# A hybrid decoder layer in one kernel: pair splits inside the next attention step, tied side sums, tied index score units, and query doubling on ScalarE

## The chip, the cores and the metric

The kernel runs on one core of a Trainium2 chip. A core has TensorE (PE, with its weight loads shown apart as PEld), VectorE (DVE), ScalarE (ACT), GpSimd (POOL) and SyncE (SP), which here issues the transfers. The metric is the device time of one execution in microseconds (us).

## The reference, cut to what matters

One decoder layer on `x` of 1024 tokens by 1024 channels, all in float32: a modulated norm, one wide input projection, sparse attention with an index that picks 256 keys for each query, retention, a gated merge, an output projection, and a gated feed-forward of width 2816.

```python
h = _rmsnorm(x, norm1_w) * (1.0 + scale1) + shift1
proj = jnp.dot(h, w_in)
(qa, ka, va, iq, ik, iw, qr, kr, vr, gr, ga, gb) = jnp.split(proj, ...)
...
# index: 8 heads of 64, blocks of 128 queries
s_h = jnp.einsum('bqhd,bsd->bqhs', iqb, ikf) * idx_scale
score = jnp.einsum('bqh,bqhs->bqs', iwb * w_scale, jax.nn.relu(s_h))
score = jnp.where(causal[None], score, NEG)
_, idx = lax.top_k(score, topk)
...
logits = jnp.einsum('bqhd,bqkhd->bqhk', qb, kg) * att_scale
p = jax.nn.softmax(jnp.where(valid[:, :, None, :], logits, NEG), axis=-1)
att = jnp.einsum('bqhk,bqkhd->bqhd', p, vg)
y_a = jnp.dot(att, w_attn_proj)
ret = _retention(_rotate(qr), _rotate(kr) * HEAD_DIM_RK ** -0.5, vr)
y_r = jnp.dot(jax.nn.silu(gr) * _head_groupnorm(ret, gn_w), w_ret_proj)
merged = jax.nn.sigmoid(ga) * y_a + jax.nn.sigmoid(gb) * y_r
x = x + gate1 * jnp.dot(merged, w_out)
...
ffn = jnp.dot(jax.nn.silu(jnp.dot(h2, w_ffn_gate)) * jnp.dot(h2, w_ffn_up), w_ffn_down)
x = _rmsnorm(x + gate2 * ffn, final_norm_w)
```

## The kernel before

**Products.** Each float32 operand of a large product is split in two parts of a reduced type, `hi` by a ScalarE copy and `lo` by a subtraction on GpSimd or VectorE, and a product is three matmuls: hi·hi, hi·lo, lo·hi. Weights are split by `split_weight` (L77 `whi`, L80 `wlo`), after a load by SyncE into `wraw`; `rows_slot` loads and splits one slot of 128 rows. `mm_tok` (lines L126, L128, L129) makes the three matmuls for each of the eight slots of a token tile of 128 rows. The later stages add and subtract blocks of the operands first and so save some products; the sums that this takes on the weights are the "side sums" (`raws` in `early_factors`, L1601, and `dw` of the down projection, L1771).

**Order.** A scheduler orders the instructions of every engine by priority and readiness; each engine then runs its own queue in that order. `turns_after(a, b)` ties `a` behind `b` on their engine without a wait. `in_line` ties each of the attention's instructions behind the one written before it on the same engine.

**The index score stage (about 104 to 213 us).** For each block of 128 queries from the third on, and for two groups of four heads, the queries `iqk` are doubled into `iqd` (L590: one half by VectorE, one by GpSimd; a single buffer), transposed on TensorE (L593) into a PSUM tile `tr`, and split to `qst` (L595 ScalarE, L596 VectorE). A score unit is a pair of matmuls for one head and up to 512 keys (L603, L604) into one of three `lg` banks; ScalarE takes the relu into one of three `rl` (L607) and VectorE adds it to the score (L611). There are 80 units. They are tied among the products of the projection of V, unit `11 * (8 t + k) // 8 - 16` behind product k of tile t, and the last ones are left to the scheduler. VectorE also makes the modulation there (`macc`, L704 and L706, fed by loads `mw`). Behind V follows the q, k projection of retention: eight tiles, each with four ScalarE copies `qk` (L833) and rotations by GpSimd (L840 to L846), and then retention's value tiles (`vs`, L902), with weight slots of their own.

**The attention (about 818 to 921 us).** The steps go over four pairs of heads, four steps each. In step d TensorE makes the logits of step d (L1315, `lga`) and, among them, five groups of transposes of the probabilities of step d − 1 (L1399, `tra`, two banks; copied to `pt` by ScalarE L1404, the third group by VectorE L1402), then the products with V (L1419, `pva`). VectorE takes the maxima (L1318), ScalarE the exponentials (L1327). When a pair's last step is through, its two output halves `pva` are split: `aT_hi` (L1423, ScalarE) and `aT_lo` (L1424, VectorE), both halves at once, directly behind the products.

**The merge (about 925 to 970 us).** For eight output blocks `nt`, products `ya` and `yb`, VectorE's gate products `sg` (L1512) and sums `merged` (L1513); then `split_merged` (`mhi` L1542, `mlo` L1543) and the products with `w_out`, whose sums VectorE adds to `x1` (L1631). After token tile 2 of the first half, `early_factors` loads and prepares the first blocks of the feed-forward's weights, with four VectorE subtractions (L1601).

**The down projection.** Products of the feed-forward's `c` (L1013, L1713: made on VectorE from the accumulators) run between those of its weights; a list `todo` of side sums (L1771) is emptied two tasks per step of the sequence.

## Time and profile before

| | us |
|---|---|
| median of three runs | 1700.72 |
| lowest, highest | 1698.78, 1701.47 |
| the profiled execution, own time | 1701.26 |
| its span | 1699.3 |
| granted TensorE clock, mean | 0.998 |
| TensorE busy | 1665.2 (98%) |
| VectorE busy | 1223.5 (72%) |
| GpSimd busy | 863.9 (51%) |
| ScalarE busy | 754.9 (44%) |

A row of the timeline gives start, duration, engine, line, operation, the tiles out<-in with their size, how many in a row, and in brackets how long the engine stood idle before it and what ended that. TensorE's matmuls are pipelined: each 128x512 matmul shows some 0.39 us but the next starts 0.23 us behind it.

### The profile page before, as it was taken

Reading aid. Unit: us, or ns where it says so; the run is one execution under the profiler, and the core shown is the slowest. Engines: PE = TensorE matmul, PEld = TensorE weight load, DVE = VectorE, ACT = ScalarE, POOL = GpSimd, SP = SyncE. Lnnn points to the kernel's source line nnn. Section 1 sums busy time; section 2 is a strip of 40 time slices with the busy share of each in tenths; the row PEclk is TensorE's granted clock in tenths of the full one; section 3 lists DMA queues with packets and bytes.
Section 4 is the critical chain, followed back from the end, with each engine's and each line's share of the span. In section 5 each row is a group of like instructions: output and inputs, shape, how many; then the busy total and the mean of one; then the engine's idle time right before and its main releaser. Section 6 shows DMA issues by size and latency. Waiting matters only on the chain.

```text
span 1699.3 us, 24532 instructions
## 1 busy us (share of the span) xinstructions
PE 1665.2 (98%) x8275; PEld 1388.9 (82%) x8275; DVE 1223.5 (72%) x2045; ACT 754.9 (44%) x1464; POOL 863.9 (51%) x854
## 2 busy tenths in 40 slices
PE   7999999999999999999999999999999999999998
PEld 5887878888888887888888788888888888888887
DVE  7639797897995779885665857966655566687674
ACT  4635533343553444431686246633333333445444
POOL 4581294793442787040355730145455545666673
PEclk9999999999999999999999999999999999999999
DMA  9454505512432464963854710235544443676652
GB/s 305 165 175 135 159 26 151 168 43 65 127 124 94 137 189 156 330 161 144 194 127 168 285 47 1 69 118 178 182 143 143 166 144 137 212 277 228 208 159 100
DMA packets 178654, 260.71 MB, mean 153 GB/s; under 512 B 13712, under 2 KB 109408, under 8 KB 176224
## 3 DMA queue, kind: packets, MB, share of 16 engines
q1 hardware_dynamic: 178272, 258.85, 48.6%
q8 instruction: 65, 1.06, 0.2%
q14 instruction: 61, 0.50, 0.1%
q10 hardware_dynamic: 256, 0.30, 0.1%
HBM read 192.51 MB, written 66.58 MB: 152 GB/s over the span
## 4 chain that ended last, share of the span: by engine, by line
PE 85%; DVE 6%; DMA 3%; ACT 2%; issue 2%; POOL 1%; SPq 0%; POOLq 0%; DVEq 0%; ACTq 0%
PE ya L1032 4%; PE ya L1030 4%; PE ya L1034 4%; PE mm L128 4%; PE mm L129 4%; PE mm L126 4%; PE yb L1030 3%; PE yb L1034 3%; PE yb L1032 3%; PE ya L1915 3%; PE ya L1913 3%; PE ya L1914 3%; PE mm L1034 2%; PE mm L1030 2%; PE mm L1032 2%
## 5 line engine op out<-in xcount | busy, mean ns | idle before, releaser
L80 POOL TENSOR_TENSOR wlo<-wraw,whi 128x512 fp32r<-128x512 f32 (+1 forms) x93 | 127.7, 1385 | 123.5 <-ACT whi L77 118.7
L642 DVE TENSOR_SCALAR_CACHE_REDUCE eq<-score,cand 128x384 uint8<-128x384 f32 (+2 forms) x192 | 180.9, 942 | 3.7
L945 POOL TENSOR_TENSOR flo<-tmp,fhi 128x512 fp32r<-128x512 f32 x79 | 107.9, 1366 | 140.5 <-ACT fhi L944 98.5
L126 PE MATMUL mm<-whi,hT_hi 128*128 128x512 f32 (+1 forms) x408 | 156.2, 388 | 1.8 <-ACT qk L833 1.8
L128 PE MATMUL mm<-wlo,hT_hi 128*128 128x512 f32 (+1 forms) x408 | 154.8, 381 | 0.5 <-DVE wlo L80 0.5
L129 PE MATMUL mm<-whi,hT_lo 128*128 128x512 f32 (+1 forms) x408 | 154.0, 380 | 0.0
L1030 PE MATMUL ya<-hc,fhi 128*128 128x512 f32 x344 | 133.8, 390 | 1.4 <-DVE c L1013 1.4
L1032 PE MATMUL ya<-hc,fhi 128*128 128x512 f32 x344 | 133.9, 389 | 0.6 <-DVE hc L1550 0.6
L1034 PE MATMUL ya<-hc,flo 128*128 128x512 f32 x344 | 132.9, 389 | 0.0
L1889 ACT ACTIVATE dslot<-draw 128x512 fp32r<-128x512 f32 x143 | 84.6, 627 | 91.8 <-DMA draw<-act_d 30.4
L945 POOL TENSOR_TENSOR flo<-raws,fhi 128x512 fp32r<-128x512 f32 x60 | 87.0, 1456 | 73.0 <-ACT fhi L944 37.9
L1890 DVE TENSOR_TENSOR dslot<-draw,dslot 128x512 fp32r<-128x512 f32 x81 | 88.9, 1133 | 45.4 <-ACT dslot L1889 45.1
L1890 POOL TENSOR_TENSOR dslot<-draw,dslot 128x512 fp32r<-128x512 f32 x62 | 95.7, 1561 | 49.8 <-ACT dslot L1889 42.0
L944 ACT ACTIVATE fhi<-tmp 128x512 fp32r<-128x512 f32 x82 | 51.5, 629 | 111.5 <-PE ya L1032 57.2
L1030 PE MATMUL yb<-hc,fhi 128*128 128x512 f32 x256 | 99.6, 389 | 0.0
L1032 PE MATMUL yb<-hc,fhi 128*128 128x512 f32 x256 | 99.6, 389 | 0.0
L1034 PE MATMUL yb<-hc,flo 128*128 128x512 f32 x256 | 99.4, 389 | 0.0
L77 ACT ACTIVATE whi<-wraw 128x512 fp32r<-128x512 f32 (+1 forms) x94 | 55.7, 609 | 92.1 <-DMA wraw<-in_w_in_dram 39.1
L998 DVE TENSOR_TENSOR tmp<-raws 128x512 f32<-128x512 f32 x40 | 30.6, 768 | 87.0 <-POOL flo L945 87.0
L126 PEld LDWEIGHTS mm<-whi,hT_hi 128*128 128x128 f32 x408 | 76.9, 189 | 13.6 <-ACT qk L833 2.2
L128 PEld LDWEIGHTS mm<-wlo,hT_hi 128*128 128x128 f32 x408 | 77.2, 189 | 12.5 <-DVE wlo L80 0.7
L129 PEld LDWEIGHTS mm<-whi,hT_lo 128*128 128x128 f32 x408 | 76.9, 189 | 12.7
(477 smaller groups left out, 4909.9 us busy)
## 6 DMA issues: line engine op xcount, KB each, us to landing
draw<-act_d SPq DMA_DIRECT2D x70, 256.0 KB
mw<-in_w_ada_dram SPq DMA_DIRECT2D x32, 512.0 KB
act_d<-c SPq DMA_DIRECT2D x58, 256.0 KB
raw<-in_w_in_dram SPq DMA_DIRECT2D x26, 512.0 KB
raws<-in_w_ffn_gate_dram SPq DMA_DIRECT2D x24, 512.0 KB
raws<-in_w_ffn_up_dram SPq DMA_DIRECT2D x24, 512.0 KB
dw<-in_w_ffn_down_dram SPq DMA_DIRECT2D x22, 512.0 KB
dw_d<-dw SPq DMA_DIRECT2D x10, 1024.0 KB
```

What stands on the lines that cost most here:

```text
L77: last_split[0] = ins = nc.scalar.activation(hi[:, :n], raw[:, :n], AF.Copy)
L80: low = (low_eng or nc.gpsimd).tensor_sub(lo[:, :n], raw[:, :n], f32(hi[:, :n]))
L126: ins = nc.tensor.matmul(ps, lhsT=ahi, rhs=whi[:, :n], start=(i == 0), stop=False)
L128: nc.tensor.matmul(ps, lhsT=ahi, rhs=wlo[:, :n], start=False, stop=False)
L129: nc.tensor.matmul(ps, lhsT=alo, rhs=whi[:, :n], start=False, stop=(i == last))
L642: ins = [nc.vector.tensor_scalar(eq[:, :sc.shape[1]], sc, thr[j], None, op0=op, op1=ALU.add, accum_out=cnt[:, j:j + 1]) for j, sc in enume ...
L945: return ins, (eng or nc.gpsimd).tensor_sub(lo, src, f32(hi))
L1030: mm = nc.tensor.matmul(ps, lhsT=whi[:, k, :], rhs=hhi[:, k, :], start=own and k == 0, stop=False, skip_group_check=True)
L1032: nc.tensor.matmul(ps, lhsT=whi[:, k, :], rhs=hlo[:, k, :], start=False, stop=False, skip_group_check=True)
L1034: nc.tensor.matmul(ps, lhsT=wlo[:, k, :], rhs=hhi[:, k, :], start=False, stop=k == 3, skip_group_check=True)
L1889: nc.scalar.activation(slot[:, 0], raw, AF.Copy)
L1890: ins = lo_eng.tensor_sub(slot[:, 1], raw, f32(slot[:, 0]))
```

## The change

Five edits, none of which alters a value that is computed:

1. `iqd` is written by one ScalarE copy of 128x512 in place of the two copies of 128x256 on VectorE and GpSimd.
2. The rule that ties score units behind products runs on into the first tile of the q, k projection, for all units left. Three of that projection's weight slots are issued ahead of V's tiles, the high parts of slots 6 and 7 are tied behind two of the last relus, and those of the first retention value slots behind the copies of q, k tile 2.
3. The attention's splits of a finished pair are written into the next step's plan: `aT_hi` of the two halves (H0, H1) behind the first and the second group of transposes, `aT_lo` (L0, L1) behind the third group and behind the second block of maxima (LB1).
4. `mlo` and the four side sums of `early_factors` are tied behind the merges and behind the additions to `x1`, and `early_factors` is called at token tile 5 in place of 2.
5. The `dw` side sums are tied behind the last additions too, and the last four products of the sequence issue no tasks.

```diff
-            for u, eng in enumerate((nc.vector, nc.gpsimd)):
-                eng.tensor_copy(iqd[:, :, u, :], iv[:, 4 * g:4 * g + 4])
+            nc.scalar.activation(iqd, iv[:, 4 * g:4 * g + 4].unsqueeze(2).to_broadcast([P, 4, 2, HD]), AF.Copy)
...
+    def qk_slot(hp, k):
+        return rows_slot([(w_in, C_QR + 256 * hp, 256), (w_in, C_KR + 256 * hp, 256)], k,
+                         behind=relus[4 * k - 37] if hp == 0 and k > 5 else None)
+
+    first_qk = [qk_slot(0, k) for k in range(3)]
+    def behind_units(mm, t, k):
+        n = 11 * (KT * t + k) // 8 - 16
+        if n >= 0:
+            turns_after(mm, units[min(n, len(units) - 1)])
...
-            mm_tok(ps, hT.lhs(t), slots)
+            for k in range(KT):
+                mm = mm_tok(ps, hT.lhs(t), slots, ks=(k,))
+                if hp == 0 and t == 0:
+                    behind_units(mm, NT, k)
...
-        slots = [rows_slot([(w_in, C_VR + 2 * DV * hp, 2 * DV)], k, low_behind=turned if k > 4 else None)
+        slots = [rows_slot([(w_in, C_VR + 2 * DV * hp, 2 * DV)], k, low_behind=turned if k > 4 else None,
+                           behind=copied if hp == 0 else None)
...
-            in_line(nc.scalar.activation(aT_hi[p][:, ds], pv, AF.Copy), 2)
-            in_line(nc.vector.tensor_sub(aT_lo[p][:, ds], pv, f32(aT_hi[p][:, ds])), 1)
+            ended.append((aT_hi[p][:, ds], aT_lo[p][:, ds], pv))
...
-        plan = T + V if d == len(steps) else (T[:1] + LB0 + T[1:3] + EB0 + LB1 + T[3:] + EB1 + LS0 + LS1 + ES0 + ES1
-                                              + RB1 + RS0 + RS1 + V)
+        plan = T + V if d == len(steps) else (T[:1] + H0 + LB0 + T[1:2] + H1 + T[2:3] + L0 + EB0 + LB1 + L1 + T[3:] + EB1
+                                              + LS0 + LS1 + ES0 + ES1 + RB1 + RS0 + RS1 + V)
...
-    def split_merged(t, gs=(0, 1)):
+    def split_merged(t, gs=(0, 1), behind=None):
...
+            if behind is not None:
+                turns_after(ins, behind)
...
-                nc.vector.tensor_sub(raw[:, :, P:], raw[:, :, P:], raw[:, :, :P])
+                turns_after(nc.vector.tensor_sub(raw[:, :, P:], raw[:, :, P:], raw[:, :, :P]), behind[2 * p + u])
...
-            mm_tok(head[t], split_merged(t, (0,)), slots, ks=range(4))
+            mm_tok(head[t], split_merged(t, (0,), merges[min(4 + t, KT - 1)]), slots, ks=range(4))
...
-                if t == 2:
-                    early_factors()
+                if t == 5:
+                    early_factors((merges[4], merges[5], added[3], added[5]))
...
-                turns_after(nc.vector.tensor_sub(*(dws[p][:, i, :] for i in (to, x, y))), fenv.added)
+                ins = nc.vector.tensor_sub(*(dws[p][:, i, :] for i in (to, x, y)))
+                for last in [fenv.added, *flow[-1].added.values()]:
+                    turns_after(ins, last)
...
+        if i >= len(seq) - 4:
+            return
```

TensorE's row at the end of the V projection and the start of retention's q, k projection; `mm` is the projection's accumulator, `lg` a score unit's. Before, the last products ahead of the end of the units, the last three units, and the first product behind them:

```order
L126 MATMUL mm<-whi,hT_hi_119 128x512
L128 MATMUL mm<-wlo,hT_hi_119 128x512
L129 MATMUL mm<-whi,hT_lo_120 128x512
L603 MATMUL lg<-khi,qst 128x512
L604 MATMUL lg<-klo,qst 128x512
L603 MATMUL lg<-khi,qst 128x512
L604 MATMUL lg<-klo,qst 128x512
L603 MATMUL lg<-khi,qst 128x512
L604 MATMUL lg<-klo,qst 128x512
L126 MATMUL mm<-whi,hT_hi_119 128x512
```

and after, the last unit but one, and the last, with the products between and behind them:

```order
L602 MATMUL lg<-khi,qst 128x512
L603 MATMUL lg<-klo,qst 128x512
L126 MATMUL mm<-whi,hT_hi_119 128x512
L128 MATMUL mm<-wlo,hT_hi_119 128x512
L129 MATMUL mm<-whi,hT_lo_120 128x512
L126 MATMUL mm<-whi,hT_hi_119 128x512
L128 MATMUL mm<-wlo,hT_hi_119 128x512
L129 MATMUL mm<-whi,hT_lo_120 128x512
```

Before, the three units stand together behind two whole q, k tiles; now the last units stand singly among the first tile's products, and the last one ahead of the products of slots 6 and 7 of that tile.

ScalarE's row at the start of the score stage; `whi` are weight splits, `vst` the V tile's copy, `rl` the relus. Before:

```order
L595 ACTIVATE qst<-tr 128x512
L77 ACTIVATE whi<-wraw 128x512 x2
L776 ACTIVATE vst<-mm 128x512
L595 ACTIVATE qst<-tr 128x512
L607 ACTIVATE rl<-lg 128x384
L77 ACTIVATE whi<-wraw 128x512
```

and after:

```order
L594 ACTIVATE qst<-tr 128x512
L589 ACTIVATE iqd<-iqk 128x512
L77 ACTIVATE whi<-wraw 128x512 x2
L785 ACTIVATE vst<-mm 128x512
L594 ACTIVATE qst<-tr 128x512
L589 ACTIVATE iqd<-iqk 128x512
L606 ACTIVATE rl<-lg 128x384
L77 ACTIVATE whi<-wraw 128x512
```

Each copy `iqd` stands directly behind the `qst` of the group before it.

ScalarE's row in the attention step behind a finished pair; `sx` and `sxs` are the exponentials, `pt` the transposed probabilities. Before:

```order
L1327 ACTIVATE sxs,mx<-sxs,mx 128x128 x2
L1423 ACTIVATE aT_hi<-pva 128x512 x2
L1404 ACTIVATE pt<-tra 128x512 x2
L1327 ACTIVATE sx,mx<-sx,mx 128x896
L1404 ACTIVATE pt<-tra 128x512
```

and after:

```order
L1343 ACTIVATE sxs,mx<-sxs,mx 128x128 x2
L1420 ACTIVATE pt<-tra 128x512
L1449 ACTIVATE aT_hi<-pva 128x512
L1420 ACTIVATE pt<-tra 128x512
L1449 ACTIVATE aT_hi<-pva 128x512
L1343 ACTIVATE sx,mx<-sx,mx 128x896
L1420 ACTIVATE pt<-tra 128x512
```

The first copy `pt` moved ahead of both splits, the second between them and the step's first exponential.

## The prediction

> **What bounds the kernel now.** I read the page first: busy times, then the chain that ended last.

> ```profile
> PE 1665.2 (98%) x8275; PEld 1388.9 (82%) x8275; DVE 1223.5 (72%) x2045; ACT 754.9 (44%) x1464; POOL 863.9 (51%) x854
> PE 85%; DVE 6%; DMA 3%; ACT 2%; issue 2%; POOL 1%; SPq 0%; POOLq 0%; DVEq 0%; ACTq 0%
> ```

> TensorE (PE) is busy 98% of the span and carries 85% of the chain; the change takes away none of its matmuls. So a gain can only come from the places where TensorE stands still: 1699.3 − 1665.2 = 34 us, part of it at start-up and the end. Next, the view of the waits, for TensorE alone (waited for: total us, times, longest us):

> ```profile
> PE tra L1399 <- ACT pt L1404: 2.6, 5, 0.9
> ...
> PE tr L593 <- DVE iqd L590: 2.4, 2, 1.9
> ...
> PE mm L1034 <- POOL wlo L945: 1.8, 1, 1.8
> PE mm L126 <- ACT qk L833: 1.8, 1, 1.8
> PE tra L1399 <- DVE pt L1402: 1.7, 4, 0.5
> PE ya L1030 <- DVE c L1013: 1.4, 2, 1.0
> PE lg L603 <- ACT rl L607: 1.2, 1, 1.2
> ...
> PE yb L139 <- DVE sg L1512: 0.3, 1, 0.3
> ```

> All but one of these rows (wlo L945, in a stretch whose order the change leaves alone) is a wait at a place where the change alters the order. They sum to 11.4 us, so that is about the most there is. Five edits, five terms; I went to the timeline at each.

> **Term a, the score stage: queries doubled by ScalarE (ACT).** Twelve pairs of copies to `iqd`, half on VectorE (DVE), half on GpSimd (POOL), become twelve ScalarE copies of 128x512. The timeline at the largest hole, the windows of the stage (the numbers behind the length are busy us of PE, PEld, DVE, ACT, POOL), and the page's row for a ScalarE copy of that size:

> ```profile
> 117.47 0.60 ACT L595 ACTIVATE qst<-tr 128x512 fp32r<-128x512 f32 x1 [1.37 <-PE tr L593]
> 118.23 1.51 DVE L706 SCALAR_TENSOR_TENSOR macc<-mw,colT,macc 128x1024 f32<-128x1024 f32 x1 [0.23 <-DMA mw<-in_w_ada_dram]
> 118.88 0.39 PE L129 MATMUL mm<-whi,hT_lo 128*128 128x512 f32 x1
> 119.67 1.39 DVE L590 COPY iqd<-iqk 128x256 f32<-128x256 f32 x1
> 121.09 0.69 DVE L596 TENSOR_TENSOR qst<-tr,qst 64x512 fp32r<-64x512 f32 x1
> 121.21 0.63 PE L593 MATMUL tr<-ident,iqd 128*128 128x128 f32 x4 [1.93 <-DVE iqd L590]
> ...
> 148.57 0.38 PE L603 MATMUL lg<-khi,qst 128*128 128x256 f32 x1 [1.16 <-ACT rl L607]
> 120.00:140.00 20.00, 18.26 (x92) 15.16 (x93) 17.79 (x28) 12.37 (x25) 5.73 (x8) 1.00 0.56 177
> 140.00:160.00 20.00, 18.84 (x105) 15.88 (x104) 19.75 (x37) 11.28 (x27) 3.17 (x4) 1.00 0.42 132
> L77 ACT ACTIVATE whi<-wraw 128x512 fp32r<-128x512 f32 (+1 forms) x94 | 55.7, 609 | 92.1 <-DMA wraw<-in_w_in_dram 39.1
> ```

> At 118.23 a 1.51-us addition of the modulation's sum holds VectorE; the copy `iqd` comes behind it at 119.67 and takes 1.39; TensorE waits 1.93. After the change the copy stands behind `qst` on ScalarE: 117.47 + 0.60 + 0.61 = 118.68, before TensorE is through with its product of 118.88. What is late next is the lower half of `qst` (0.69) on VectorE, still behind the addition: 118.23 + 1.51 + 0.69 = 120.43. The score unit that reads it then starts some 0.9 us late. The gain there is about 1.2 of 2.1. At the other of the two waits on `iqd` (2.4 − 1.9 = 0.5) I count it all. At 148.57 the wait for a relu goes back to VectorE, whose load in that window is 19.75 of 20; taking copies away from it helps, while ScalarE gets more: I count 0.3 of 1.16. Cost on ScalarE: 12 × 0.61 = 7.3 us over the 50 us from 115 to 161, beside 12.37 and 11.28 busy us of 20, so it lies in its idle time. Term a: 2.0. Ends: +3.5 (the three waits of 1.93, 0.5 and 1.16 all gone) and, since a single `iqd` buffer makes every group's transposes wait for a copy in ScalarE's queue behind relus, below nothing: that is priced among the rivals.

> **Term b, the last ten score units tied into the first q, k tile.** Before, three units stand one behind the other and the next tile's product comes after them. The timeline, and the windows around 213 and around a wait of the same length at 655 (PEclk is the third number from the end):

> ```profile
> 212.52 1.57 ACT L607 ACTIVATE rl<-lg 128x512 f32<-128x512 f32 x3 [1.18 <-PE lg L604]
> 213.00 0.39 PE L604 MATMUL lg<-klo,qst 128*128 128x512 f32 x1
> 213.97 2.19 ACT L833 ACTIVATE qk<-mm,rscale 128x128 f32<-128x128 f32 x8
> 215.18 0.50 PE L126 MATMUL mm<-whi,hT_hi 128*128 128x512 f32 x1 [1.78 <-ACT qk L833]
> 215.20 2.56 POOL L840 TENSOR_TENSOR rra<-qk,cosr 128x512 f32<-128x512 f32 x1 [11.08 <-ACT qk L833]
> ...
> 216.47 0.63 PE L129 MATMUL mm<-whi,hT_lo 128*128 128x512 f32 x1
> ...
> 219.46 0.56 PE L126 MATMUL mm<-whi,hT_hi 128*128 128x512 f32 x1
> 216.00:219.60 3.60, 3.60 (x11) 2.80 (x10) 3.50 (x9) 0.57 (x3) 3.60 (x5) 0.55 0.51 150
> 655.00:657.30 2.30, 0.48 (x4) 0.06 (x2) 2.26 (x6) 0.22 (x1) 2.30 (x3) 1.00 0.49 164
> 657.30:661.00 3.70, 3.70 (x16) 3.09 (x17) 3.70 (x7) 2.28 (x5) 3.70 (x3) 1.00 0.78 235
> 254.20 3.80 POOL L80 TENSOR_TENSOR wlo<-wraw,whi 128x512 fp32r<-128x512 f32 x3
> ```

> ScalarE owes three relus and then the eight `qk` copies of two tiles (2.19); the product at 215.18 needs an accumulator that only these copies free. TensorE, done at 213.00 + 0.23, restarts at 215.18: 1.95 lost. In the new order the last units stand among the products of the first tile, whose copies then come behind few relus, and each later tile (24 products × 0.23 = 5.5 us) gives ScalarE time for four copies (1.1). The wait goes; nothing else on ScalarE is late there. Behind the wait the clock fell: 0.55 in that window, and the seven steps from 216.47 to 219.46 took 2.99 us where 16 matmuls in 3.70 us (0.23 each) would make it 1.61, so 1.4 more. Whether this comes back is not certain: the stop at 655 was as long (1.8 in the waits) and cost no clock. I take it as tied to the pause, since it starts 1.3 us behind it and no other stretch of this stage has it. Term b: 1.95 + 1.4 = 3.4. Ends: 1.5 (the pause only, with 0.4 left) and 3.7.

> [...]

> The same edit puts the first tile's rotation on GpSimd a tile earlier, and some low parts of retention's first weights (L80, 1.27 each by the row of three) between the rotations instead of behind them. Before, GpSimd had these three to do at 254.20, behind the rotations that start at 215.20: 39 us for eight tiles, 4.9 each, against 5.5 on TensorE. The earlier start pays for about 5.5 us of low parts put in between, so I expect no wait of the value tiles; a rival below prices it.

> **Term c, the attention pairs' splits.** Windows of one ordinary step and of two steps in which a finished pair is split, and the split:

> ```profile
> 858.11:864.61 6.50, 6.50 (x68) 5.75 (x67) 4.28 (x16) 4.79 (x11) 2.28 (x4) 1.00 0.89 208
> 864.61:872.64 8.03, 6.72 (x67) 5.75 (x66) 5.47 (x19) 6.44 (x16) 4.20 (x5) 1.00 1.02 218
> 892.30:900.48 8.18, 6.84 (x70) 5.82 (x70) 5.75 (x21) 6.58 (x17) 4.22 (x6) 1.00 0.12 42
> 867.81 1.06 ACT L1423 ACTIVATE aT_hi<-pva 128x512 fp32r<-128x512 f32 x2
> ```

> The latter two are 1.53 and 1.68 longer than the first, and TensorE stands idle for 1.31 and 1.34 of it, because both `aT_hi` (1.06 together) stand on ScalarE ahead of both `pt` copies, and both `aT_lo` on VectorE ahead of the logits' maxima. Three such steps lose nearly 4 us together (the two rows of `pt` waits in the first view, 4.3, hold them and some of the last step). After, one `pt` comes ahead of each `aT_hi`, and each `aT_lo` stands behind a `pt` or a maximum. But ScalarE's work in those steps, 6.44 and 6.58, is about the whole of an ordinary step, so not all closes: a step can come down to about 6.8–7.0. Term c: 0.5 + 2 × 1.0 = 2.5; ends 1.0 and 3.5. The last pair's splits stand behind the last step as before: nothing.

> **Terms d and e, the side sums.** The window of the merges that TensorE waits for with one of the side sums, and the down stage:

> ```profile
> 957.01 1.78 DVE L1601 TENSOR_TENSOR raws<-raws 128x512 f32<-128x512 f32 x1
> 958.00:970.00 12.00, 11.33 (x48) 8.56 (x47) 12.00 (x15) 1.26 (x2) 8.84 (x7) 1.00 0.62 234
> 1479.26 1.19 DVE L1771 TENSOR_TENSOR dw<-dw 128x512 f32<-128x512 f32 x1
> 1480.37 1.77 DVE L1713 TENSOR_TENSOR c<-c,c 128x512 f32<-128x512 f32 x1
> 1482.79 0.50 PE L1030 MATMUL ya<-hc,fhi 128*128 128x512 f32 x1 [1.04 <-DVE c L1013]
> ```

> In d VectorE works 12 of 12 us and TensorE loses 0.67. Tied behind the merges, four sums of 1.78 (7.1 us) leave its path; the sums' loads and splits come later, and what needs them (the feed-forward's first blocks) lies far behind. Term d: 0.7, ends 0 and 1.3. In e, one `dw` sum of 1.19 ends just before the subtraction that makes `c`; without it that comes 1.19 earlier and the wait of 1.04 closes. The sums are made some microseconds later, ahead of weights that are not read until tens of microseconds on. Term e: 1.0, ends 0 and 1.35.

> **Sum.** 2.0 + 3.4 + 2.5 + 0.7 + 1.0 = 9.6. From this I take 1.2 for new short waits, since at most of the five places the order of a second engine changes as well: 8.4. The profiled execution took 1701.26 (0.54 above the median of 1700.72), so 1701.26 − 8.4 = 1692.9 for such a one, and 1692.5 as a median, rounded.

> **The rivals.**
> Half comes back: the holes move to another wait. For it: VectorE at 19.75 of 20 around 150, ScalarE at 6.5 us in a pair's step; also the GpSimd chain, where low parts that come 2 to 5 us late would hold retention's first value tile and eat term b. Against: of the five terms, b and e remove the one thing TensorE waits for. It gives 3 to 5 us, about 1697.
> Slower: ScalarE becomes the pacer of the score stage. With one `iqd` buffer, each of the 12 groups' transposes can come behind one copy and one relu (0.61 + 1.57/3 = 1.13): 12 × 1.13 = 13.6 lost, against 7.6 from b to e: 6 us slower, 1706.7. It decides from (7.6 + 3.4)/12 = 0.92 us per group. Against it: ScalarE idles 8 of 20 us there, and the copies of a group can run a whole group of units before they are read.
> The clock's part stays: the pause goes, but the clock falls all the same for 1.4 us somewhere in the stage, as it did not fall behind the equal stop at 655. The time is then 1692.5 + 1.4 = 1693.9; against it, the drop follows the only long pause of that stage within 1.3 us. One in four within the first case.
> No effect: the units, splits and sums are tied, but the lost time turns up one wait later at each: 1700.5. TensorE's 98% speaks for it in that other holes exist; yet none of the five holes has a second wait of the same length beside it in the rows.

> **How the numbers follow.** Most closes, 1688 to 1696.5: 0.62 (0.47 with the clock's part, 0.15 without). Half, 1695 to 1699.5: 0.24. Slower: 0.09. No effect: 0.05. A measurement of this kernel can tell about 0.2%, 3.4 us, from no change: faster is below 1697.3, slower above 1704.1. The first case and half of the second: 0.74 faster; the other half and no effect: 0.17 same; 0.09 slower. The range: the low end is the sum with terms a, b, c at their upper ends and no allowance, 1.5 + 0.3 + 1.0 + 1.2 = 4.0 more gain, 1688.5, and one more for d and e: 1687.5; the high end takes in the second case and no effect: 1700.5.

> **What the profile after would show.** Right: no wait of a transpose on `iqd` above 0.3; no pause and no clock below 0.9 around 213; pair steps under 7.0; no wait on `sg`; no wait on `c` near 1480. Wrong: waits of `tr` on ScalarE, a `vs` or `mm` wait near 255 on GpSimd's low parts, VectorE's `qst` as the new wait, the clock drop at another place. The forecast falls if the twelve groups wait on ScalarE, or if more than one of the holes b and c returns under another name.

## The result, and the profile after

The changed kernel takes 1692.19 us, median of five runs (1688.83 to 1692.76), against 1699.95 before (1698.78 to 1701.47): a ratio of 0.9949, 95% interval 0.9935 to 0.9964. The forecast was 1692.5. The profiled execution is the quickest of the five, 1688.83, and that of before, 1701.26, would lie near the top of the five of before; so the two profiles lie 12.4 us apart and the medians 7.8. What follows goes by stages and by more than one profile for that reason.

The page of after, busy times and chain:

```profile
span 1687.0 us, 24500 instructions
PE 1660.5 (98%) x8275; PEld 1387.4 (82%) x8275; DVE 1214.1 (72%) x2033; ACT 760.5 (45%) x1476; POOL 857.3 (51%) x842
PE 86%; issue 5%; DVE 4%; DMA 2%; ACT 1%; POOL 1%; SPq 0%; POOLq 0%; DVEq 0%; ACTq 0%
```

The counts are as the diff says: VectorE and GpSimd 12 instructions fewer, ScalarE 12 more, TensorE the same. The view of TensorE's waits, after:

```profile
PE lg L602 <- ACT rl L606: 2.3, 2, 1.9
...
PE mm L1050 <- POOL wlo L961: 1.8, 1, 1.8
PE ya L1954 <- DVE c L1750: 0.9, 1, 0.9
PE tra L1415 <- ACT pt L1420: 0.9, 3, 0.3
...
PE lg L602 <- DVE qst L595: 0.3, 1, 0.3
PE lg L1046 <- DVE kept L1029: 0.3, 1, 0.3
PE tra L1415 <- DVE pt L1418: 0.3, 1, 0.3
```

Gone are the waits on `iqd`, on `qk`, on `sg`, on the modulation's `macc`, and most of those on `pt` (4.3 to 1.2 in all). New are a wait of 1.9 for a relu, one of 0.9 on `c` at another product, and a short one on `kept`. Nearly gone is a wait for a relu near 147: 1.16 us in before, 0.35 in after. TensorE waited 11.4 us in the rows that the prediction summed; the rows in their place come to some 5.

A table of stretches, worked out from the starts of TensorE's matmuls in the timelines, one execution each. Stretch 1 goes from the index projection's first matmul (128x292) to the attention's first logits in `lga`, 2 from there to the first transpose of the second norm (so attention and merge), 3 on to the first down product, 4 to the last matmul. The labels are those of the experiments below.

| kernel | 1 | 2 | 3 | 4 |
|---|---|---|---|---|
| before | 753.76 | 208.65 | 453.06 | 216.54 |
| before_again | 753.17 | 207.17 | 453.04 | 216.60 |
| after | 748.24 | 203.51 | 453.05 | 216.42 |
| after_again | 749.00 | 203.47 | 453.08 | 216.76 |
| no_query | 749.75 | 203.82 | 453.10 | 216.45 |
| no_units | 750.53 | 203.44 | 453.09 | 216.46 |
| no_units_again | 749.50 | 203.39 | 453.08 | 216.46 |
| no_ab | 752.83 | 203.44 | 453.04 | 216.40 |
| no_att | 749.68 | 206.93 | 453.09 | 216.43 |
| no_side | 749.40 | 204.80 | 453.14 | 216.48 |
| no_down | 750.27 | 203.49 | 453.04 | 216.53 |
| fix1 | 748.04 | 203.46 | 453.07 | 216.71 |
| fix12 | 749.41 | 203.49 | 453.04 | 215.80 |
| fix12_noq | 748.90 | 203.74 | 453.04 | 216.20 |

By the means of the two profiles each, the change gained 4.8 in stretch 1 (753.47 to 748.62), 4.4 in stretch 2 (207.91 to 203.49), and nothing in 3 and 4 (216.57 to 216.59 in the last). That is 9.2 where the medians say 7.8 and, in the second comparison, 8.5; both profiles of before hold a drop of the clock, in stretch 1, of some 1.6 us (last section) that need not come in every execution. Ahead of stretch 1 the start differs by up to 1.5 us between executions (58.7 to 60.2), whatever the kernel.

### The profile page after: what moved, and what is told of

It reads as the page before. It is cut to its first block, busy times and chain, and to the rows that moved or that the text cites. A ratio compares the mean times of both kernels' runs of the same rounds, so it can differ in the third digit from the quotient of the medians.

```text
span 1687.0 us, 24500 instructions
## 1 busy us (share of the span) xinstructions
PE 1660.5 (98%) x8275; PEld 1387.4 (82%) x8275; DVE 1214.1 (72%) x2033; ACT 760.5 (45%) x1476; POOL 857.3 (51%) x842
## 3 DMA queue, kind: packets, MB, share of 16 engines
q8 instruction: 65, 1.06, 0.3%
## 4 chain that ended last, share of the span: by engine, by line
PE 86%; issue 5%; DVE 4%; DMA 2%; ACT 1%; POOL 1%; SPq 0%; POOLq 0%; DVEq 0%; ACTq 0%
PE ya L1048 4%; PE ya L1046 4%; PE ya L1050 4%; PE mm L128 4%; PE mm L129 4%; PE mm L126 4%; PE yb L1046 3%; PE yb L1050 3%; PE yb L1048 3%; PE ya L1955 2%; PE ya L1954 2%; PE ya L1956 2%; PE mm L1050 2%; PE mm L1048 2%; PE mm L1046 2%
## 5 line engine op out<-in xcount | busy, mean ns | idle before, releaser
L80 POOL TENSOR_TENSOR wlo<-wraw,whi 128x512 fp32r<-128x512 f32 (+1 forms) x93 | 126.8, 1379 | 153.0 <-ACT whi L77 137.0
L126 PE MATMUL mm<-whi,hT_hi 128*128 128x512 f32 (+1 forms) x408 | 155.3, 384 | 0.0
L129 PE MATMUL mm<-whi,hT_lo 128*128 128x512 f32 (+1 forms) x408 | 153.9, 378 | 0.0
L77 ACT ACTIVATE whi<-wraw 128x512 fp32r<-128x512 f32 (+1 forms) x94 | 55.8, 611 | 90.8 <-DMA wraw<-in_w_in_dram 37.7
L129 PEld LDWEIGHTS mm<-whi,hT_lo 128*128 128x128 f32 x408 | 76.7, 188 | 12.1
L126 PEld LDWEIGHTS mm<-whi,hT_hi 128*128 128x128 f32 x408 | 76.5, 188 | 11.4 <-ACT gstage L295 0.3
```

What stands on the lines that cost most here:

```text
L77: last_split[0] = ins = nc.scalar.activation(hi[:, :n], raw[:, :n], AF.Copy)
L80: low = (low_eng or nc.gpsimd).tensor_sub(lo[:, :n], raw[:, :n], f32(hi[:, :n]))
L126: ins = nc.tensor.matmul(ps, lhsT=ahi, rhs=whi[:, :n], start=(i == 0), stop=False)
L129: nc.tensor.matmul(ps, lhsT=alo, rhs=whi[:, :n], start=False, stop=(i == last))
```

## The experiments

All but the last were timed in five rounds beside the kernel before.

| kernel | median, us | ratio to before, 95% interval |
|---|---|---|
| after_again | 1691.86 | 0.9942, 0.9930 to 0.9955 |
| no_query | 1692.21 | 0.9948, 0.9936 to 0.9961 |
| no_units | 1692.38 | 0.9951, 0.9939 to 0.9964 |
| no_att | 1693.97 | 0.9962, 0.9949 to 0.9976 |
| before_again | 1699.01 | 0.9998, 0.9987 to 1.0009 |
| no_side | 1693.27 | 0.9963, 0.9950 to 0.9975 |
| no_down | 1692.21 | 0.9958, 0.9944 to 0.9971 |
| fix1 | 1689.94 | 0.9940, 0.9928 to 0.9952 |
| fix12 | 1689.59 | 0.9931, 0.9919 to 0.9944 |
| fix12_noq | 1692.65 | 0.9948, 0.9935 to 0.9962 |
| no_ab | 1694.10 | 0.9958, 0.9946 to 0.9971 |
| no_units_again | 1690.47 (one execution) | |

The rows from after_again to no_att were timed beside a median of 1700.41 for before, those from before_again to fix1 beside 1699.52, the last ones beside 1701.67. So across these groups compare ratios rather than medians; 0.001 of a ratio is 1.7 us. An interval is some 4 us wide, and that of after (0.9935 to 0.9964) overlaps those of all the changed kernels; only no_att's five runs (1693.84 to 1695.11) all lie above those of after and after_again. For the others the stretches and the waits must tell.

**after_again: the changed kernel once more.**

> The changed kernel once more, for a second profile. Theory 1 (the profiled execution of after was on the quick side by its start-up and its clock, not by the five places): the holes at the five places return within 0.3 us, among them the new one in the score stage near 188 us (2.1) and the one near 1478 us (1.1), and the time is 1690 to 1693. Theory 2 (the new hole near 188 us comes and goes with the transfers): it is absent or shorter than 1 us in this execution, or another one stands elsewhere in the stage.

Theory 1 holds: the stop near 190 us is there again (1.77 of wait), so is that on `c` at 1481 (1.27). It is made by the order, and this is how it comes about, in after's timeline:

```profile
181.14 7.99 POOL L80 TENSOR_TENSOR wlo<-wraw,whi 128x512 fp32r<-128x512 f32 x3 [57.52 <-ACT whi L77]
186.03 2.73 SPq L101 DMA_DIRECT2D wraw<-in_w_in_dram  x4
189.88 0.63 ACT L77 ACTIVATE whi<-wraw 128x512 fp32r<-128x512 f32 x1 [3.50 <-DMA wraw<-in_w_in_dram]
190.41 1.56 ACT L606 ACTIVATE rl<-lg 128x512 f32<-128x512 f32 x3
191.05 0.50 PE L602 MATMUL lg<-khi,qst 128*128 128x512 f32 x1 [1.90 <-ACT rl L606]
```

There are three buffers `wraw`, and a buffer comes free when its low part is made. Of the three low parts in the first row the first takes 4.86 us (181.14 to 186.00), the other two 1.48 and 1.73, so the next loads go out only at 186.03, behind a wait of 5.0 for that low part. The high part of slot 6, tied behind the thirteenth relu from the end, waits for its load 3.50 us on ScalarE, the relus stand behind it in ScalarE's queue, and TensorE stops until one of them has freed an `lg` bank.

**no_query: term a undone** (VectorE and GpSimd double the queries again).

```diff
-            nc.scalar.activation(iqd, iv[...].unsqueeze(2).to_broadcast([P, 4, 2, HD]), AF.Copy)
+            for u, eng in enumerate((nc.vector, nc.gpsimd)):
+                eng.tensor_copy(iqd[:, :, u, :], iv[:, 4 * g:4 * g + 4])
```

> After with the queries doubled by VectorE and GpSimd again, the four other edits kept. Theory 1 (each edit closes its own wait): TensorE waits for iqd again, some 2 us in the score stage come back, 1.5 to 3 us slower than after. Rival (ScalarE was loaded by the doubling, and the wait for a relu behind a weight split near 188 us is its price): that wait shrinks by 1 us or more, and the time is that of after within 1 us.

The waits on `iqd` return (1.8 in two), so does that for a relu near 146 (1.16, against 0.35), and the wait for a relu near 192 falls from 1.8 or 1.9 to 1.2. Stretch 1 is 1.1 longer than the mean of after, the time 0.35, inside its scatter. Both theories have a part: the doubling closes waits of its own, and 0.6 to 0.7 of that was paid at the new stop.

**no_units: term b undone** (no ties of the last units to the q, k tile, no early slots, no ties of high parts).

```diff
-    first_qk = [qk_slot(0, k) for k in range(3)]
+    first_qk = []
...
-                if hp == 0 and t == 0:
-                    behind_units(mm, NT, k)
```

> After without the ties of the last score units, the early q, k slots and the ties of retention's first splits. Theory 1: the three units stand together again, TensorE stops 1.9 us for the qk copies and the clock falls behind the stop for about 1.4 us more; the hole near 188 us (2.1), which a weight split tied ahead of its load makes, goes. Net 1 to 2 us slower than after. Rival (the clock's drop is not the stop's): the stop is there at full clock, and the net is 0 or less.

The stop of 1.9 for `qk` is back, that near 190 is gone, and the wait on `macc` near 334 (1.1) is back too. The clock did not fall. TensorE's windows from the stop on, no_units (PEclk third from the end):

```profile
210.60:212.78 2.18, 0.40 (x3) 0.00 (x1) 2.02 (x4) 2.18 (x8) 0.00 (x0) 1.00 0.00 0
212.78:214.30 1.52, 1.52 (x7) 1.26 (x8) 1.52 (x4) 0.98 (x4) 1.50 (x1) 1.00 0.00 0
214.30:216.00 1.70, 1.70 (x9) 1.43 (x8) 1.63 (x5) 0.00 (x0) 1.70 (x2) 1.00 0.59 99
```

So the rival on the clock is right for this run, while the net, +0.5 in time and +1.9 in stretch 1, has the sign of theory 1. In the second profile of the same kernel, no_units_again, stretch 1 is 0.9 longer than in after, and the wait on `macc` 0.6.

**no_att: term c undone** (both splits directly behind the products again).

```diff
-            ended.append((aT_hi[p][:, ds], aT_lo[p][:, ds], pv))
+            in_line(nc.scalar.activation(aT_hi[p][:, ds], pv, AF.Copy), 2)
+            in_line(nc.vector.tensor_sub(aT_lo[p][:, ds], pv, f32(aT_hi[p][:, ds])), 1)
```

> After with both splits of a finished attention pair directly behind its products again. Theory 1: the three steps behind a pair take 7.4 to 8.2 us again instead of 6.6 to 6.9; 3 to 4 us slower than after. Rival (the steps were near ScalarE's own time, and part of the gain came from elsewhere): 1 to 2 us slower.

Stretch 2 grows by 3.4 us (203.49 to 206.93), the time by 2.1. Windows of a step behind a pair and the step after it, no_att and then after:

```profile
859.67:867.71 8.04, 6.74 (x67) 5.76 (x67) 5.61 (x20) 6.45 (x16) 4.20 (x5) 1.00 1.04 220
867.71:874.22 6.51, 6.51 (x67) 5.71 (x66) 4.50 (x18) 5.82 (x15) 4.40 (x6) 1.00 0.61 136
```

```profile
856.92:863.36 6.44, 6.44 (x68) 5.78 (x67) 4.49 (x16) 6.19 (x16) 4.21 (x5) 1.00 1.02 218
863.36:870.26 6.90, 6.62 (x67) 5.75 (x66) 5.47 (x22) 6.01 (x15) 4.25 (x6) 1.00 0.80 176
```

The step behind the pair has no stop left at all; ScalarE works 6.19 of its 6.44 us. The three such steps took 7.53, 8.04 and 8.05 us in no_att and 6.43 each in after. Some 0.4 comes back in the step behind the second and the third, where a `pt` is late by 0.3 (the row of 0.9 in three waits, above). The steps and the stretch say theory 1; the time, 2.1, lies between the two.

**before_again: two equal kernels.**

> The kernel before, once more, for a second profile and for the scatter of two equal kernels. Theory 1 (the clock's drop behind 213 us is not made by the stop there, since the stop at 210.6 us in after without the unit ties had none): the stop of 1.9 us is there again and the clock stays at 1.00 behind it, or drops elsewhere. Rival (the drop belongs to the stop in this order): 0.55 again behind the stop, some 1.4 us. The ratio to before is 1 within 0.15%.

The ratio is 0.9998. The stop is there and so is the drop of the clock, 1.1 us behind its end (1.2 in the first profile):

```profile
211.50:213.71 2.21, 0.43 (x2) 0.01 (x1) 2.02 (x4) 2.21 (x8) 0.00 (x0) 1.00 0.00 0
213.71:215.00 1.29, 1.29 (x5) 1.09 (x6) 1.29 (x3) 0.98 (x4) 1.26 (x1) 0.94 0.00 0
215.00:216.50 1.50, 1.50 (x5) 1.11 (x5) 1.43 (x6) 0.00 (x0) 1.50 (x2) 0.50 0.49 60
```

That spoke for the rival, until no_ab and no_units_again below. Two waits on which the prediction built were not the same here: the longest on `iqd` was 0.84, not 1.93, and there was none on `sg`.

**no_side: term d undone.**

```diff
-            mm_tok(head[t], split_merged(t, (0,), merges[min(4 + t, KT - 1)]), slots, ks=range(4))
+            mm_tok(head[t], split_merged(t, (0,)), slots, ks=range(4))
...
-                turns_after(nc.vector.tensor_sub(raw[:, :, P:], raw[:, :, P:], raw[:, :, :P]), behind[2 * p + u])
+                nc.vector.tensor_sub(raw[:, :, P:], raw[:, :, P:], raw[:, :, :P])
...
-                if t == 5:
+                if t == 2:
```

> After without the ties of mlo and of the four side sums, early_factors back at token tile 2. Theory 1 (the merges' waits on VectorE close by these ties alone): the stretch from the last pva product to the first normalized transpose is 1.4 to 1.8 us longer than in after, so is the time. Rival (it closes because the attention's splits leave VectorE earlier): under 0.5 us.

Stretch 2 is 1.3 longer (204.80), the time 1.1 to 1.4 (2.4 to 3.6 by the ratios): theory 1, in the stretch a little under its size. A wait on `sg` returns to TensorE's view (0.3). But before_again, which has no such ties either, does not lose this time: from the last product `pva` to the second norm's first transpose TensorE takes 101.82 us in before and 101.66 in no_side, yet 100.30 in before_again, as in after (100.32). VectorE's four side sums in before_again, and GpSimd's row beside the second:

```profile
945.51 1.78 DVE L1601 TENSOR_TENSOR raws<-raws 128x512 f32<-128x512 f32 x1
950.61 0.68 DVE L1601 TENSOR_TENSOR raws<-raws 128x512 f32<-128x512 f32 x1
950.67 5.17 POOL L1612 TENSOR_TENSOR wraw<-wraw,gate 128x512 f32<-128x512 f32 x3 [0.53 <-DMA wraw<-in_w_out_dram]
954.61 1.78 DVE L1601 TENSOR_TENSOR raws<-raws 128x512 f32<-128x512 f32 x1
957.51 0.68 DVE L1601 TENSOR_TENSOR raws<-raws 128x512 f32<-128x512 f32 x1
```

In before each of the four took 1.78 or 1.82. So without the ties the sums cost the merges 1.3 to 1.5 us in two profiles and nothing in a third; in all eleven profiles with the ties they cost nothing.

**no_down: term e undone** (the `dw` sums placed as before).

```diff
-                for last in [fenv.added, *flow[-1].added.values()]:
+                for last in [fenv.added]:
...
-        if i >= len(seq) - 4:
-            return
```

> After with the dw side sums placed as before. Theory 1 (the edit only moved the wait of about 1 us from a product of the feed-forward to a product of the down projection, behind c and its accumulator): the time is that of after within 0.5 us, with one wait of 1.0 on c at a feed-forward product and none at a down product. Rival (the edit gained its 1.0): 1 us slower.

Theory 1: stretch 4, where this edit acts, is 216.53 against 216.42 and 216.76. By the ratio, 0.9958, the kernel is 1.5 to 2.7 us slower than after, within the intervals; the drop of the clock in this profile lies in stretch 1. VectorE and the waiting product in no_down,

```profile
1469.96 1.18 DVE L1808 TENSOR_TENSOR dw<-dw 128x512 f32<-128x512 f32 x1
1471.06 1.77 DVE L1750 TENSOR_TENSOR c<-c,c 128x512 f32<-128x512 f32 x1
1472.76 0.67 DVE L1029 TENSOR_TENSOR c<-c,ya 128x512 f32<-128x512 f32 x1
1473.49 0.50 PE L1046 MATMUL ya<-hc,fhi 128*128 128x512 f32 x1 [1.04 <-DVE c L1029]
```

and in after:

```profile
1476.86 1.78 DVE L1808 TENSOR_TENSOR dw<-dw 128x512 f32<-128x512 f32 x1
1478.56 0.67 DVE L1750 TENSOR_TENSOR c<-c,ya 128x512 f32<-128x512 f32 x1
1479.29 0.50 PE L1954 MATMUL ya<-dslot 128*128 128x512 f32 x1 [0.93 <-DVE c L1750]
```

The sums left the way of one reader of VectorE and stand in the way of the next: the gating product L1750, which frees the accumulator `ya` for a down product.

**fix1: slots 6 and 7 split three relus later.**

```diff
-                         behind=relus[4 * k - 37] if hp == 0 and k > 5 else None)
+                         behind=relus[4 * k - 34] if hp == 0 and k > 5 else None)
```

> After with the high parts of q, k slots 6 and 7 tied three relus later (behind the tenth and the sixth relu from the end in place of the thirteenth and the ninth). Theory 1 (near 188 us ScalarE waits 3.5 us for the load of slot 6, and the relus behind it hold the score units' accumulators): the hole of 2 us near 188 goes, no other comes in the stage, 1.5 to 2 us faster than after. Rival (the relus are late there by VectorE, or the stage ends on another wait): the hole stays above 1 us or turns up within 15 us of it; same time as after.

The stop near 190 us is gone and none comes in its stage: the last score matmul starts 89.8 us behind the first `iqd` transpose, against 91.6 in after and 92.1 in after_again. Yet stretch 1 is only 0.6 shorter (748.04 against 748.62), as most of it is lost again near 485, in fix1's timeline:

```profile
479.10 6.14 POOL L961 TENSOR_TENSOR wlo<-wraw,whi 128x512 fp32r<-128x512 f32 x2 [35.88 <-ACT whi L960]
484.04 1.76 DVE L1014 TENSOR_TENSOR wraw<-raw 128x512 f32<-128x512 f32 x1 [1.18 <-POOL wlo L961]
485.71 0.68 DVE L1029 TENSOR_TENSOR kept<-kept,lg 128x512 f32<-128x512 f32 x1
486.44 0.50 PE L1046 MATMUL lg<-hT_hi,whi 128*128 128x512 f32 x1 [1.50 <-DVE kept L1029]
```

VectorE waits for GpSimd's low part with `kept` behind it, and TensorE for `kept`: 1.5 us here, 0.3 and 0.7 in the two profiles of after, 0 and 0.3 in those of before. That it is longer because the score stage ends sooner is not shown: no_side, whose score stage is that of after, has 1.1. The median, 1689.94, is 1.9 below that of after_again, but the ratios, 0.9940 and 0.9942, are all but equal.

**fix12: that, and the last `dw` sums behind the gating product as well.**

```diff
-                nc.vector.tensor_mul(a, a, src)
+                fenv.gated = nc.vector.tensor_mul(a, a, src)
...
-                for last in [fenv.added, *flow[-1].added.values()]:
+                for last in [fenv.added, *flow[-1].added.values(), *([fenv.gated] if p >= NP - 3 else [])]:
```

> After with both corrections: the high parts of q, k slots 6 and 7 three relus later, and the dw side sums of the last three pairs tied behind the last gating product on VectorE too. Theory 1 (the wait near 1478 us is the gating product, held behind two dw sums of 1.78 us on VectorE, and it holds the accumulator that the next down product needs): the wait on c there falls below 0.2 us, 1 us faster than with the first correction alone, about 1689. Rival (the wait moves again, to the down slots' low parts, which now follow each other on VectorE): a wait of 0.7 us or more on dslot, no gain.

The wait on `c` falls to 0.2 and stretch 4 to 215.80, 0.8 below the mean of after and 0.9 below fix1: theory 1 for the wait. The time, 0.35 below fix1's, does not show the 1 us. TensorE's waits on `kept` and `c` in fix12:

```profile
PE lg L1046 <- DVE kept L1029: 1.4, 1, 1.4
...
PE ya L1954 <- DVE c L1750: 0.2, 1, 0.2
```

At 1689.59, ratio 0.9931, it is the quickest kernel here; it beats before beyond its interval; that it beats after (0.9942 and 0.9949) is likely and not shown, since the intervals overlap.

**fix12_noq: fix12 with the queries doubled by VectorE and GpSimd.**

> The kernel with both corrections, but the queries doubled by VectorE and GpSimd. Theory 1 (the doubling on ScalarE is worth what the waits on iqd cost, 0.8 + 1.3 + 1.3 us less the waits of 0.4 to 0.9 that stand in their place): 1 to 2 us slower than with both corrections. Rival (what is gained ahead of 480 us is given back where TensorE waits for GpSimd's chain there): within 0.5 us, with a longer wait near 485 in the quicker one.

1692.65 against 1689.59 has the sign of theory 1 and more than its size; the intervals overlap. In stretch 1 the two single profiles say the opposite, 748.90 against 749.41. The score stage itself settles it: from V's first product to the first transpose of a rotated query tile (`rq`) TensorE takes 109.38 us in fix12_noq and 106.88 in fix12, so the doubling is worth 2.5 there. The waits that make most of it, in fix12_noq and then what is left in fix12:

```profile
128.69 0.63 PE L593 MATMUL tr<-ident,iqd 128*128 128x128 f32 x4 [1.21 <-DVE iqd L590]
147.28 0.38 PE L603 MATMUL lg<-khi,qst 128*128 128x256 f32 x1 [1.15 <-ACT rl L607]
```

```profile
145.86 0.45 PE L602 MATMUL lg<-khi,qst 128*128 128x384 f32 x1 [0.35 <-ACT rl L606]
```

Behind the stage fix12's profile loses 3.0 again, 1.6 by a drop of the clock (last section) and 0.9 by the longer wait on `kept` (1.4 against 0.5). That longer wait is the sign that the rival named, but one pair of profiles does not show that it follows from the quicker stage.

**no_ab: terms a and b undone together** (both diffs above).

> After with both the query doubling and the ties of the score units undone; the attention and the side sums as changed. Theory 1 (the terms add): 5 us of gain are left, so 1694 to 1695.5, 3 us slower than after, though each of the two alone cost 0.4 and 0.5 us, because in those the hole near 188 us went or shrank. The clock's drop behind the stop near 213 us returns, if it belongs to this order. Rival (single undoings show all there is): 1692.5 to 1693.5 and no drop.

Stretch 1 is 4.2 longer than in after, the time 2.2 (1.5 to 2.7 by the ratios): in the stretch theory 1, and more than the sum of the two alone (1.1 and 1.4, the latter the mean of two). Alone, each undoing also took away some of the stop that b had made, and the other edit's gain went on. TensorE also waits 1.6 for `macc` here, 0.8 to 1.0 in before. The clock stayed at 1.00 behind a stop of 1.8 at the same place and in the same order as in before:

```profile
211.80:213.98 2.18, 0.39 (x2) 0.00 (x1) 2.03 (x4) 2.18 (x8) 0.00 (x0) 1.00 0.00 0
213.98:215.50 1.52, 1.52 (x7) 1.24 (x8) 1.52 (x4) 0.98 (x4) 1.49 (x1) 1.00 0.00 0
215.50:218.50 3.00, 3.00 (x15) 2.47 (x14) 2.88 (x8) 0.50 (x2) 3.00 (x5) 1.00 0.61 180
```

**no_units_again: the same kernel as no_units, for the clock.**

> After without the unit ties, a second profile, for the clock alone. Theory 1 (whether the clock drops behind the stop of 1.9 us is a matter of when it falls): either outcome, with a drop in about half. Rival (the drop belongs to the order of before): full clock behind the stop again.

Full clock behind the stop again. With no_ab that is three executions with the stop at 210 to 214 and no drop. So the order around the stop does not bring the drop by itself.

## Why the prediction was right, and where it was not

The total was right, 1692.19 for 1692.5. The mechanism was right for a to d: the waits that the terms named closed. That the number came so near is partly luck, for the terms missed to both sides. Of the signs that it set itself, that of no wait on `c` near 1480 failed; the others came true, beside a new wait of 0.3 on `qst`.

- **Term a, 2.0.** The mechanism was right: the copy is ready ahead of its transposes and what is late next is the lower half of `qst`, as predicted (the wait of 0.3 on `qst` in after). Undone alone it is worth 1.1 in stretch 1; where the new stop near 190 is out of the way, 2.5 in the score stage (fix12 and fix12_noq). The parts differ from the sum: the wait of 1.93 on which it was built was 0.6 to 0.9 at that place in the four other profiles with these copies, while of the relu's 1.16 it counted 0.3 and 0.8 went.
- **Term b, 3.4.** The pause of 1.95 went. The clock's 1.4 (1.6, measured against no_ab) went in both profiles of after, but it was too large as a term, for here the clock fell behind 4 of 25 such pauses (below); no_down and fix12, with the pause gone, lost it at another stop. So the third rival, that the clock falls all the same, came true in some executions, though in a later stage. Two parts were not in the sum: the wait on `macc` near 337 went as well (0.8 and 1.0 in before), which lay in no term; and the stop near 190 (1.8 to 1.9) came. The prediction allowed 1.2 for new waits of all kinds, and looked for them at GpSimd's chain behind 254, where none came. It costed the early slots at nothing and did not name ScalarE's queue behind a high part that waits for its load. That step failed. With it and `kept` (0.3 to 0.7), new waits cost about 2.5.
- **Term c, 2.5.** It measured 3.4 by no_att, close to the upper end. The prediction held that ScalarE's 6.44 us of work would keep such a step at 6.8 or more; that failed. ScalarE works 6.19 of 6.44 us, and the step lost its stops entirely, since the copies that TensorE needs stand first.
- **Term d, 0.7.** It measured 1.3 by no_side, the upper end, and 1.5 against before, but nothing against before_again, where the wait was absent without the edit. The prediction took the idle time of one window, 0.67, of one execution.
- **Term e, 1.0.** It measured nothing. The step that failed is that taking one sum of 1.19 from ahead of `c` closes the wait: VectorE ran without a gap there, and the sums only went from one wanted result to the next. fix12 shows what it took, and its worth, 0.8.
- **The sum.** a and b together measured 4.8 in stretch 1 against before, of which 1.6 is the clock's drop, and 4.2 against no_ab (predicted 5.4, less the allowance); c and d 4.4 to 4.7 (3.2), e 0 (1.0).

Of the rivals, "ScalarE becomes the pacer" did not happen through `iqd`; a part of its mechanism, relus behind other work in ScalarE's queue, did, at one place. "Half comes back" happened in part, at 190, 485 and 1479, which the upper ends of c and d made up for.

## What to carry to other kernels

In after a split of a weight whose load was not yet there stood 3.50 us on ScalarE, with the relus in the queue behind it, and TensorE lost 1.90: tie such a split to a place behind which its load has landed, and reckon the load from the moment its buffer comes free (186.03 there, 3.85 ahead of the split at 189.88). Moving work out of the way of one result gained nothing where the next result on that engine was wanted at once (term e: 0, and 0.8 in fix12, where the sums left the way of both); look at who waits for the two instructions behind the gap. And take the medians from runs and the causes from stretches of several profiles, two of the unchanged kernel among them: here two single profiles differed by 12.4 us where the kernels differ by 8, and two waits that were to be closed were shorter or absent in the second profile of the same kernel.

## What the runs showed of the hardware

The clock. In the fourteen profiles TensorE lost 1.77 to 2.21 us at one stop (from start to start of its matmuls, less 0.23) 25 times behind the first 100 us. Four of these stops were followed by 3.41 us at half clock: before and before_again near 215, no_down and fix12 near 651. It began 0.6 to 1.2 us behind the restart. It cost some 1.6 us: from the restart near 651 to the next transposes of weights TensorE takes 36.20 and 36.23 us in no_down and fix12, and 34.59 to 34.63 in the other twelve; from the last score matmul to the first transpose `rq`, 10.28 and 10.32 in before and before_again, and 8.71 in no_ab with the same order. Windows of fix1, and then fix12, behind the same stop:

```profile
651.74:653.00 1.26, 1.26 (x5) 1.05 (x6) 1.26 (x3) 0.44 (x1) 1.26 (x2) 1.00 0.52 192
653.00:656.00 3.00, 3.00 (x15) 2.48 (x14) 3.00 (x5) 2.42 (x5) 3.00 (x3) 1.00 0.81 233
```

```profile
650.70:652.00 1.30, 1.30 (x5) 1.04 (x6) 1.30 (x3) 0.43 (x1) 1.30 (x2) 0.97 0.53 191
652.00:655.00 3.00, 3.00 (x8) 2.32 (x7) 3.00 (x5) 2.46 (x5) 3.00 (x3) 0.50 0.90 244
```

```profile
646.77:650.18 3.41, 3.17 (x14) 2.28 (x13) 3.34 (x7) 0.89 (x2) 3.41 (x3) 1.00 0.36 121
650.18:653.59 3.41, 1.85 (x8) 1.55 (x9) 3.41 (x7) 0.64 (x2) 3.41 (x4) 1.00 0.66 225
```

```profile
648.50:651.91 3.41, 1.60 (x7) 1.02 (x6) 3.37 (x8) 0.63 (x1) 3.41 (x4) 1.00 0.52 177
```

In fix1 the stop lies across two steps, in fix12 inside one. It lay inside one step, whole or but for 0.05 us, in 7 of the 25 cases, with TensorE busy for 47 to 48% of the step; four of these seven were followed by the drop, and none of the other 18, where TensorE was busy for over half of each step. Why three of the seven kept the full clock is open. In these profiles a stop of 2 us cost, beside itself, 4/25 × 1.6 = 0.3 us on average, and not 1.6.

GpSimd beside VectorE: VectorE's four side sums of 128x512 took 1.78 to 1.82 us in before, with GpSimd busy all the while; in after two took 1.78 with GpSimd busy all the while, one 1.00 with GpSimd busy for 0.46 of it, and one 0.69 with GpSimd idle. In before_again the second took 0.68 from 950.61 on, with GpSimd's next row at 950.67 (no_side, above). GpSimd's low part of 128x512 took 1.29 to 1.30 in before at 254, with VectorE busy for 3.73 of the 3.80 us of all three, and, in after at 181, 4.86, 1.48 and 1.73, with VectorE busy all the while. A price of 1.27 us for one low part, taken from the row at 254, was a quarter of what the first one came to where the early slots were put. What made that one so long was not shown: VectorE was busy beside the short ones too, and no run here changed the work of one of the two engines alone.
